# Holding VectorE and ScalarE to program order through the projections of a hybrid decoder step

## The chip, the cores and the metric

One core of one Trainium2 chip runs the whole program in one launch. The metric is the device time of one execution in microseconds. TensorE (PE in the profile; PEld is its weight load) multiplies, VectorE (DVE) and ScalarE (ACT) do element work, SyncE (SP) issues nearly all DMAs.

## The reference

One layer of a hybrid decoder on 288 tokens: 256 of a prompt and 32 of eight sample requests (four tokens each, with 2048 cached positions). Cut to what matters here:

```python
u = rmsnorm(h, g_mix)
z = u @ w_in                                   # 2048 x 2880
c_q, c_kv, k_r, x_br, y_br = split(z)          # 512, 256, 64, 1024, 1024
q = (rmsnorm(c_q, g_q) @ w_uq)                 # 8 heads of 128 + 64
o_lat = attend(q_lat, rope(q_r), rmsnorm(c_kv, g_kv), rope(k_r))   # prompt: causal; sample: paged cache
o_mla = o_lat @ w_uv
xc = causal_conv(x_br);  o_rec = rglru(xc);  o_lru = gelu(y_br) * o_rec
h = h + concat(rmsnorm(o_mla, g_out_mla), rmsnorm(o_lru, g_out_lru)) @ w_o
h = h + hier_moe(rmsnorm(h, g_ffn))            # 32 experts, 2 of them for each token
h = h + sigmoid(rmsnorm(h, g_ple) @ w_ple_gate) * (p @ w_ple_proj)
```

All in float32.

## The kernel before

Activations lie with the feature in the partitions and the 288 tokens along the free axis. A projection in `dense3` makes one block of 128 output columns. It goes through the 2048 (or 1024) rows in pieces of 8 x 128, called **steps** here. A step's weights, 128 x 1024 numbers, come by one DMA of 512 KB into `wraw` (4 buffers). To keep the product nearly exact, both sides are held in two parts. `load_split` makes the weights' parts:

```python
nc.scalar.copy(hi[:, x, :], r[:, x, :])                                   # L222: whi, 3 buffers
nc.vector.tensor_sub(lo[:, x, :], r[:, x, :], hi[:, x, :].bitcast(F32))   # L223: wlo, 2 buffers
```

`mm3` then issues three matmuls for each of the 8 row blocks: L232 (whi by the high part, h), L233 (whi by the low part, g), L234 (wlo by the high part, l). A step has 24 matmuls; it can begin with whi alone, and its first L234 needs wlo. After the last step of a block `evac` takes the sum out of PSUM, and after each step `hook()` runs.

The projections come in this order: `w_in` in 23 blocks of two steps (4 for `cq`, 3 for `lat` and `kr`, then for each of four LRU parts 2 for `xx` and 2 for `yb`), `w_uq` in 6 steps (each with two sums of 12 matmuls), `w_o[0]` (the recurrent half) in 16 steps and `w_o[1]` (the attention half) in 16 steps. That is 84 steps. Everything else of the layer is put between them by `hook()`: it pops one entry of the list `hooks` and then calls `tick()`, which moves each running **lane** on by one stage. Hooks hold the norms of the queries (`norm_q1`, `norm_q2`), the conv, gates, decay and scan of the LRU parts (`begin`, `conv`, `gates`, `decay`, `input`, `scan`, `out`), and in `w_o[1]` the routing's sums (`post`). Lanes are the 16 units of the sample attention (`sample`: scores, maximum, exp, transposes, output) beside the LRU blocks, and then `prompt_pool` and the 8 heads of the prompt attention (`prompt`) beside `w_o[0]`. `rsqrt_of` and `spread` make a per-token scale: `ssx`, `rsv`, `rss`, `rsr`, `diag`, `spread`, then `rx` (or `ry`, `ro`). `heads_out` splits the 8 heads' outputs (`om`) into parts before `w_o[1]`.

What decides the order: the program is traced, and a scheduler then lays each engine's instructions into one fixed row by its own estimates of time, subject to the dependencies. So the row of an engine needn't be the order in which the code was written: before, the casts of the weights (L222) and the subtractions (L223) stand among the hook's work wherever the scheduler put them. On the chip each engine goes through its row strictly in order, and an instruction that waits holds up all that stand behind it.

After the projections come the routing and the experts (MoE), from about 450 us on, whose weights stream through five and more slots of 2 MB each; SP issues the loads of weights in the order of its own row.

Of the kernel before, what the change touches and what calls it, by code (L numbers as in the profile page):

```python
# [117 lines left out]
def hymba_kernel(ctx, tc, a):  # L118
    nc = tc.nc
# [62 lines left out]
    def tick():  # L182

        for g in list(lane):
            if next(g, 1):
                lane.remove(g)
        for _ in range(min(PAGES // 4, len(loads))):
            loads.pop(0)()
        if queue:
            clock[0] += 1  # L190
            if clock[0] <= AHEAD or (clock[0] - AHEAD) % PACE == 0 or clock[0] >= DENSE:
                start()

    def start():
        if queue[0][0] and lane:
            return
        g = queue.pop(0)[1]()
        lane.append(g)
        if next(g, 1):
            lane.remove(g)  # L200

    def hook():
        if hooks:
            hooks.pop(0)()
        tick()

    def load(src, n=1):
        r = wps[0].tile([128, 8, 128], F32, name="wraw", bufs=wps[1])
        for i in range(n):
            dma(r[:, 8 * i // n:8 * (i + 1) // n, :],  # L210
                src[:, 1024 * i // n:1024 * (i + 1) // n].rearrange("p (k c) -> p k c", c=128))
        return r
# [23 lines left out]
    def dense3(srcs, xh, xl, evac, pre=(), ps_=None):  # L236

        acc = (ps_ or psA)([128, NTOK], "acc")
        nq = len(pre) if srcs is None else srcs.shape[0]
        last = 8 * nq - 1  # L240
        for q in range(nq):
            r = pre[q] if q < len(pre) else None
            hi, lo = r if isinstance(r, tuple) else load_split(None if r is not None else srcs[q], r)
            for k in range(8):
                kk = 8 * q + k
                mm3(acc, hi[:, k, :], lo[:, k, :], xh(kk), xl(kk), kk == 0, kk == last)
            if q == nq - 1:
                evac(acc)
            hook()
# [78 lines left out]
    for k in range(KD):  # L328
        if k in at:
            i, h = at[k]  # L330
# [5 lines left out]
    def squares(q):  # L336
        if q == 0:
            tc.keep_in_program_order(nc.scalar.activation(acc4, xT[:, :4, :], AF.Square))
        else:
            sq4 = xs.tile([128, 4, NTOK], F32, name="sq4")  # L340
            tc.keep_in_program_order(nc.scalar.activation(sq4, xT[:, 4 * q:4 * q + 4, :], AF.Square))
            nc.vector.tensor_add(acc4, acc4, sq4)
        if q == 3:
            nc.vector.tensor_add(acc4[:, 0:2, :], acc4[:, 0:2, :], acc4[:, 2:4, :])
            nc.vector.tensor_add(accs[0], acc4[:, 0, :], acc4[:, 1, :])
            st_x.close()
# [31 lines left out]
    def ev_q(i, p):  # L378
        nc.vector.tensor_mul(cq[:, i, :], p, rx_of())
        add_sq(accs[1], tmp, cq[:, i, :], i)  # L380

    pcq = []
    hooks += [lambda: None] * NSQ + [lambda q=q: squares(q) for q in range(4)]
    hooks += [lambda: [ev_q(i, pcq[i]) for i in range(2)], lambda: [ev_q(i, pcq[i]) for i in range(2, 4)]]
    for i in range(4):
# [472 lines left out]
    while hooks:  # L858
        hook()
# [20 lines left out]
    while lane or queue:  # L880
        hook()
# [828 lines left out]
```

## Time and profile before

| | |
|---|---|
| median of 3 runs | 1489.26 us (1486.46 to 1492.16) |
| the profiled execution | 1484.32 us, its span 1482.4 us |
| mean granted clock of TensorE | 0.957 |
| PE busy | 1302.5 us, 88% of the span |
| VectorE busy | 562.0 us, 38% |
| ScalarE busy | 397.7 us, 27% |
| mean DMA rate | 350 GB/s |

The span runs from the first to the last instruction. Busy shares are averages over stages: the projections take the first 449 us, and the MoE and the gated embedding the rest. Granted clock 1.00 is the full level, 2.4 GHz; a stretch below it was in part at the half level, 1.2 GHz.

### The profile page before, as it was taken

The page shows a single profiled execution, that of the slowest core. Times are in us where ns is not written, and L with a number is a line of the kernel's source. Part 1 is how long each engine was busy: PE and PEld are TensorE (multiplying, and loading weights), DVE is VectorE, ACT ScalarE, POOL GpSimd, SP SyncE. Part 2 cuts the span into 40 slices and gives each one's busy share as a digit, 9 for nine tenths or more (in the row PEclk, how much of TensorE's full clock was granted, in tenths as well). Part 3 has the DMA queues.
Part 4 walks back from the last instruction along what each step waited for, and adds up shares of the span by engine and source line. Part 5 has one row for each costly group of instructions (what it writes and reads, how often), then busy time and mean ns, then how long its engine had stood idle before and what let it go on. Part 6 is the DMA issues. An engine that isn't in the chain of part 4 may idle for free. (4 is left out here: it accounts for less than half of the span.)

```text
span 1482.4 us, 24470 instructions
## 1 busy us (share of the span) xinstructions
PE 1302.5 (88%) x9883; PEld 857.6 (58%) x9883; DVE 562.0 (38%) x1368; ACT 397.7 (27%) x762; POOL 3.0 (0%) x9
## 2 busy tenths in 40 slices
PE   8999888899999999679778777969788999999996
PEld 7997676788996445125224322516245666666786
DVE  6765644767653011000000010103024455555676
ACT  6545533655441101001000010102013322222236
POOL 0000000000000000000000000000000000000000
PEclk9999999999999999999989988989899999999997
DMA  7879776342768899999999999999999999999971
GB/s 273 286 241 363 259 268 215 118 165 86 263 257 334 347 414 427 428 426 430 427 428 427 428 427 426 418 423 428 416 420 419 420 418 419 418 419 418 412 310 65
DMA packets 81784, 518.34 MB, mean 350 GB/s; under 512 B 9473, under 2 KB 11714, under 8 KB 50818
## 3 DMA queue, kind: packets, MB, share of 16 engines
q1 hardware_dynamic: 81010, 514.33, 86.3%
q0 software_dynamic: 656, 2.39, 0.4%
q8 instruction: 80, 1.31, 0.4%
q14 instruction: 38, 0.31, 0.1%
HBM read 513.81 MB, written 2.88 MB: 349 GB/s over the span
## 5 line engine op out<-in xcount | busy, mean ns | idle before, releaser
L1119 PE MATMUL Gp<-w,Xq 128*32 128x512 f32 (+1 forms) x1888 | 339.4, 668 | 78.5 <-DMA w<-in_w_gate 40.0
L1119 PEld LDWEIGHTS Gp<-w,Xq 128*32 128x32 f32 (+1 forms) x1888 | 84.0, 126 | 280.1 <-issue 160.6
L232 PE MATMUL acc<-uh,whi 128*128 128x288 f32 x496 | 154.6, 312 | 10.6 <-ACT whi L228 5.7
L234 PE MATMUL acc<-uh,wlo 128*128 128x288 f32 x496 | 152.1, 307 | 8.2 <-DVE ms L541 5.2
L233 PE MATMUL acc<-ul,whi 128*128 128x288 f32 x496 | 150.6, 304 | 0.4 <-DVE ul L267 0.4
L1128 DVE SCALAR_TENSOR_TENSOR Yb<-Gp,rs,Yb 128x512 f32<-128x512 f32 x10 | 7.5, 751 | 329.6 <-PE Gp L1119 288.9
L1152 PE MATMUL Y<-w,w 128*32 128x256 f32 (+2 forms) x1440 | 112.4, 360 | 20.8 <-DMA w<-in_w_down 20.8
L1169 DVE TENSOR_TENSOR hT<-hT,yp 128x288 f32<-128x288 f32 x160 | 71.4, 450 | 155.3 <-PE yp L1167 155.1
L1092 PE MATMUL xp<-Pq,hn 96*128 96x256 f32 (+1 forms) x576 | 119.3, 359 | 8.4 <-DVE Pq L1076 8.4
L1092 PEld LDWEIGHTS xp<-Pq,hn 96*128 96x128 f32 x576 | 96.8, 196 | 49.6 <-issue 39.4
L232 PEld LDWEIGHTS acc<-uh,whi 128*128 128x128 f32 x496 | 95.6, 193 | 17.7 <-ACT whi L222 5.7
L223 DVE TENSOR_TENSOR wlo<-wraw,whi 128x1024 fp32r<-128x1024 f32 x82 | 99.9, 1218 | 12.3 <-PE acc L234 6.8
L234 PEld LDWEIGHTS acc<-uh,wlo 128*128 128x128 f32 x496 | 95.7, 193 | 14.8 <-DVE wlo L223 11.2
L222 ACT CAST whi<-wraw 128x1024 fp32r<-128x1024 f32 x82 | 85.1, 1045 | 68.1 <-PE acc L233 60.5
L233 PEld LDWEIGHTS acc<-ul,whi 128*128 128x128 f32 x496 | 96.0, 194 | 2.2 <-DVE ul L267 1.3
L1152 PEld LDWEIGHTS Y<-w,w 128*32 128x32 f32 (+1 forms) x1440 | 54.9, 115 | 64.4 <-DMA w<-in_w_down 34.3
L1156 ACT ACTIVATE Yh<-Y,wsl 128x256 fp32r<-128x256 f32 (+1 forms) x90 | 40.6, 451 | 182.9 <-PE Y L1152 182.2
L1096 DVE TENSOR_SCALAR Xq<-xp,P 128x256 f32<-128x256 f32 (+1 forms) x48 | 21.1, 439 | 161.5 <-PE xp L1092 161.5
L1152 PE MATMUL Y<-w,wl 128*32 128x256 f32 (+3 forms) x864 | 71.4, 360 | 6.2 <-DMA w<-in_w_down 6.2
L1127 ACT ACTIVATE Yb<-Gp,rs 128x512 f32<-128x512 f32 x10 | 6.9, 687 | 259.5 <-PE Gp L1119 259.4
L234 PE MATMUL acc<-gh,wlo 128*128 128x288 f32 x240 | 70.8, 295 | 1.4 <-DVE wlo L229 1.4
L233 PE MATMUL acc<-gl,whi 128*128 128x288 f32 x240 | 70.9, 295 | 0.0
(482 smaller groups left out, 1882.2 us busy)
## 6 DMA issues: line engine op xcount, KB each, us to landing
w<-in_w_gate SPq DMA_DIRECT2D x63, 2048.0 KB, 28.8
w<-in_w_down SPq DMA_DIRECT2D x112, 1024.0 KB, 17.4
w<-in_w_up SPq DMA_DIRECT2D x55, 2048.0 KB, 27.8
kv<-in_cache SPq DMA_DIRECT2D x128, 288.0 KB, 5.4
wraw<-in_w_in SPq DMA_DIRECT2D x44, 512.0 KB, 5.7
hT<-in_w_up SPq DMA_DIRECT2D x9, 2048.0 KB, 29.6
wraw<-in_w_o SPq DMA_DIRECT2D x32, 512.0 KB, 3.4
wraw<-in_w_pg SPq DMA_DIRECT2D x32, 512.0 KB, 17.4
```

The costliest lines, as they stand in the source:

```text
L222: nc.scalar.copy(hi[:, x, :], r[:, x, :])
L223: nc.vector.tensor_sub(lo[:, x, :], r[:, x, :], hi[:, x, :].bitcast(F32))
L232: nc.tensor.matmul(out, hi, xh, start=start, stop=False)
L233: nc.tensor.matmul(out, hi, xl, start=False, stop=False)
L234: nc.tensor.matmul(out, lo, xh, start=False, stop=stop)
L1092: nc.tensor.matmul(xp, hn[:, t, d * 128:(d + 1) * 128], Pq[:, t, :n], start=t == 0, stop=t == 2)
L1096: nc.vector.tensor_scalar(X[:, d, :n], xp, prm("g_ffn", d), None, op0=ALU.mult)
L1119: nc.tensor.matmul(acts[j][sl * e:sl * e + sl, :], X[:, kk, o:o + sl], wt[e](k), start=kk == 0, stop=kk == KD - 1)
L1128: nc.vector.scalar_tensor_tensor(sg, acts[1], rs, sg, op0=ALU.mult, op1=ALU.mult)
L1152: nc.tensor.matmul(Y[sl * e:sl * e + sl, :], at[:, f, sl * e:sl * e + sl], w(f), start=f == 0, stop=f == 3)
L1156: nc.scalar.activation(Yh, Y, AF.Copy, scale=ws)
L1169: nc.vector.tensor_add(h_, h_, yp)
```

## The change

A new function `in_order()` is called at the end of every `hook()`. It goes through the instructions that were traced since its last call, and gives each one on ScalarE or VectorE a dependency (without a semaphore) on the one traced before it on the same engine. A call with `first=True` before the first projection starts the chain. No instruction is added, removed or altered (762 on ScalarE, 1368 on VectorE, both before and after); the two engines' rows are held to the order of the code from the first step of `w_in` to the last hook of `w_o[1]`. TensorE's and SP's rows stay with the scheduler, which lays them by what it now finds. Lines of the changed kernel are numbered 15 or 16 higher (L222 is L237, L223 is L238, L874 is L890).

```diff
+    kept, traced = {}, [0]
+
+    def in_order(first=False):
+
+        ins = nc.cur_bb.bb.instructions
+        if not first:
+            for i in ins[traced[0]:]:
+                if i.engine in (mybir.EngineType.Activation, mybir.EngineType.DVE):
+                    if i.engine in kept:
+                        tc.add_manual_dep(i, kept[i.engine].name, mybir.DependencyInfo(
+                            mybir.DependencyClass.NoSync, mybir.DependencyReason.DATA), reason="in_order")
+                    kept[i.engine] = i
+        traced[0] = len(ins)
+
     def hook():
         if hooks:
             hooks.pop(0)()
         tick()
+        in_order()
...
     pcq = []
+    in_order(True)
     hooks += [lambda: None] * NSQ + [lambda q=q: squares(q) for q in range(4)]
```

Three places show what moves. The first is VectorE's row in the middle of `w_o[1]`, two steps long (`evt` and `hT` take a block's sum out, `acch` adds squares). Before:

```order
L874 TENSOR_TENSOR evt<-acc,ro 128x288
L223 TENSOR_TENSOR wlo<-wraw,whi 128x1024
L875 TENSOR_TENSOR hT<-hT,evt 128x288
L276 TENSOR_TENSOR acch<-acch,sqa 128x288
L874 TENSOR_TENSOR evt<-acc,ro 128x288
L223 TENSOR_TENSOR wlo<-wraw,whi 128x1024
```

And of the change:

```order
L890 TENSOR_TENSOR evt<-acc,ro 128x288
L891 TENSOR_TENSOR hT<-hT,evt 128x288
L291 TENSOR_TENSOR acch<-acch,sqa 128x288
L238 TENSOR_TENSOR wlo<-wraw,whi 128x1024
L890 TENSOR_TENSOR evt<-acc,ro 128x288
L891 TENSOR_TENSOR hT<-hT,evt 128x288
```

Before, `wlo` stood right behind `evt`; now `hT` and `acch` stand between them, and `wlo` is the last of its step.

The second is ScalarE's row at the seventh to eleventh step of `w_in`, where the token scale `rx` is made, the blocks of `cq` are taken out and normed (`sqa`, `qh`). Before:

```order
L222 CAST whi<-wraw 128x1024 x3
L257 ACTIVATE rss<-rsv 96x3
L297 COPY rx<-spread 128x288
L222 CAST whi<-wraw 128x1024
L272 ACTIVATE acc_103<-cq 128x288
L275 ACTIVATE sqa<-cq 128x288 x3
L222 CAST whi<-wraw 128x1024
```

And of the change:

```order
L237 CAST whi<-wraw 128x1024
L272 ACTIVATE rss<-rsv 96x3
L312 COPY rx<-spread 128x288
L287 ACTIVATE acc_103<-cq 128x288
L290 ACTIVATE sqa<-cq 128x288
L237 CAST whi<-wraw 128x1024
L290 ACTIVATE sqa<-cq 128x288 x2
L237 CAST whi<-wraw 128x1024
```

Before, two more casts stood ahead of `rss`; now the next step's cast stands behind `rss`, `rx` and the squares of `cq`.

The third is VectorE's row beside the LRU blocks, where a step's sum is taken out (`xx`), a sample unit goes on (`Obs`, `ms`) and the next part of the conv begins (`xc`, `cvs`, `cvp`). Before:

```order
L223 TENSOR_TENSOR wlo<-wraw,whi 128x1024
L741 TENSOR_TENSOR xx<-acc,rx 128x256
L742 TENSOR_TENSOR xx<-acc,rx 128x8x4
L570 SCALAR_TENSOR_TENSOR Obs<-Obs,ms,Os 128x256
L762 COPY cvs<-xx 128x48
L763 COPY cvp<-xx 128x6
L528 TENSOR_REDUCE ms<-Ss 128x1
L767 TENSOR_SCALAR xc<-xx,P 128x312
L530 TENSOR_TENSOR ms<-ms 128x1
L770 SCALAR_TENSOR_TENSOR xc<-xx,P,xc 128x312
L541 TENSOR_SCALAR ms<-ms 128x1
L223 TENSOR_TENSOR wlo<-wraw,whi 128x1024
```

And of the change:

```order
L238 TENSOR_TENSOR wlo<-wraw,whi 128x1024
L757 TENSOR_TENSOR xx<-acc,rx 128x256
L758 TENSOR_TENSOR xx<-acc,rx 128x8x4
L586 SCALAR_TENSOR_TENSOR Obs<-Obs,ms,Os 128x256
L544 TENSOR_REDUCE ms<-Ss 128x1
L546 TENSOR_TENSOR ms<-ms 128x1
L557 TENSOR_SCALAR ms<-ms 128x1
L564 SCALAR_TENSOR_TENSOR ms<-ms 128x1
L238 TENSOR_TENSOR wlo<-wraw,whi 128x1024
```

Before, the conv's first operations stood ahead of `wlo`, and the last `ms` of the unit (L548) behind it; now the sample unit's whole chain of `ms` stands ahead of `wlo` and the conv behind it, ahead of the next step's `wlo`.

## Rows read from the trace of the kernel before

**Rows 1.** Busy time, clock and DMA by stage; first a stretch and its length.

```profile
core 0: us, PE busy (x) PEld busy (x) DVE busy (x) ACT busy (x) POOL busy (x), PEclk, DMA share, GB/s
34.00:84.50 50.50, 50.09 (x365) 48.10 (x364) 34.48 (x69) 28.00 (x60) 0.00 (x0) 1.00 0.81 275
95.10:289.70 194.60, 174.69 (x1539) 136.52 (x1531) 111.02 (x280) 90.18 (x149) 0.00 (x0) 0.97 0.71 247
309.20:384.80 75.60, 75.60 (x513) 69.28 (x513) 49.28 (x110) 36.88 (x85) 0.00 (x0) 0.98 0.28 95
449.20:520.00 70.80, 66.63 (x408) 36.58 (x407) 14.99 (x73) 9.33 (x20) 0.00 (x0) 0.95 0.91 360
520.00:1482.40 962.40, 815.93 (x6171) 453.61 (x6167) 268.52 (x667) 164.29 (x342) 2.79 (x5) 0.94 0.97 405
```

**Rows 2.** The page's chain that ended last, and its two costliest weight-part groups.

```profile
DMA w<-in_w_down 22%; DMA w<-in_w_up 2%; PE Gp L1119 2%; PE xp L1092 2%; PE Y L1152 2%; DMA wpp<-in_w_pp 1%; PE s L1507 1%; PE acc L1516 0%; DVE hT L1613 0%; PE pp L1328 0%; PE yp L1167 0%; PE acc L234 0%; PE spread L293 0%; DVE z L1527 0%; PE acc L233 0%
...
L223 DVE TENSOR_TENSOR wlo<-wraw,whi 128x1024 fp32r<-128x1024 f32 x82 | 99.9, 1218 | 12.3 <-PE acc L234 6.8
...
L222 ACT CAST whi<-wraw 128x1024 fp32r<-128x1024 f32 x82 | 85.1, 1045 | 68.1 <-PE acc L233 60.5
```

**Rows 3.** Timeline of one step's end in `w_o[1]`: start, duration, instruction.

```profile
400.65 0.29 PE L234 MATMUL acc<-uh,wlo 128*128 128x288 f32 x1
...
400.98 0.46 DVE L874 TENSOR_TENSOR evt<-acc,ro 128x288 f32<-128x288 f32 x1 [1.06 <-PE acc L234]
401.36 1.22 DVE L223 TENSOR_TENSOR wlo<-wraw,whi 128x1024 fp32r<-128x1024 f32 x1
401.85 0.29 PE L234 MATMUL acc<-uh,wlo 128*128 128x288 f32 x1
402.25 0.29 PE L234 MATMUL acc<-uh,wlo 128*128 128x288 f32 x1
402.49 0.45 DVE L875 TENSOR_TENSOR hT<-hT,evt 128x288 f32<-128x288 f32 x1
```

**Rows 4.** The two evacuations of `w_o`: count, durations in ns, first and last start.

```profile
L874 DVE TENSOR_TENSOR evt<-acc,ry x16: 448/458/458, 309.0 to 384.4; 128x288 f32<-128x288 f32 x16
L874 DVE TENSOR_TENSOR evt<-acc,ro x16: 448/458/460, 392.4 to 448.9; 128x288 f32<-128x288 f32 x16
```

**Rows 5.** Timeline of a head's softmax beside `w_o[0]`, and its transposes one step apart.

```profile
319.75 0.49 PE L659 MATMUL pt<-C,Sb 128*128 128x128 f32 x3
326.72 0.49 PE L659 MATMUL pt<-C,Sb 128*128 128x128 f32 x3
...
322.18 0.56 DVE L645 TENSOR_TENSOR Sb<-S,C 128x384 f32<-128x384 f32 x1 [0.18 <-PE S L642]
324.84 0.55 DVE L655 TENSOR_SCALAR Sb<-Sb,m 128x128 f32<-128x128 f32 x2
```

**Rows 6.** Timeline of the token scale: its first and its last instruction.

```profile
35.55 0.15 DVE L256 TENSOR_SCALAR rsv<-ssx 96x3 f32<-96x3 f32 x1
38.16 0.40 ACT L297 COPY rx<-spread 128x288 f32<-128x288 f32 x1 [2.22 <-PE spread L293]
```

**Rows 7.** Groups by line and form, VectorE and ScalarE: count, busy us, mean ns.

```profile
L528 DVE TENSOR_REDUCE ms<-Ss 128x1 f32<-128x256 f32 x15 | 6.4, 423 | 8.8 <-PE Ss L523 8.8
L770 DVE SCALAR_TENSOR_TENSOR xc<-xx,P,xc 128x312 f32<-128x312 f32 x24 | 12.9, 539 | 0.1
L267 DVE SCALAR_TENSOR_TENSOR uh<-om,P,uh 128x256 fp32r<-128x256 f32 x8 | 3.9, 484 | 0.5 <-ACT uh L266 0.5
L542 ACT ACTIVATE Ssb<-Ss,ms 128x256 f32<-128x256 f32 x16 | 7.6, 475 | 38.8 <-DVE ms L541 34.3 <-DVE sp L723 4.4
L446 ACT COPY qrs<-qrT 64x32 f32<-64x32 f32 x16 | 3.5, 216 | 0.2
```

**Rows 8.** Two stretches of 10 us in which TensorE had gaps.

```profile
190.00:200.00 10.00, 8.23 (x66) 7.37 (x65) 4.24 (x11) 2.63 (x5) 0.00 (x0) 0.83 0.70 257
230.00:240.00 10.00, 6.66 (x63) 4.72 (x64) 3.28 (x10) 3.97 (x8) 0.00 (x0) 1.00 0.85 287
```

## The prediction

> **What bounds the kernel now.** I read the table by stage first, then the chain, then timelines inside the projections. The chain that ended last is made of the experts' weights (`w<-in_w_down` 22%) [rows 2]: behind the projections the span is set by a stream of weights, at 405 GB/s from 520 us on and 360 in the first 71 us [rows 1]. The projections are the other kind of stage. In their four large stretches TensorE is busy for 50.1 of 50.5, 174.7 of 194.6 and 75.6 of 75.6 us, while VectorE has 34.5, 111.0 and 49.3 and ScalarE less [rows 1]. So TensorE is the bound there, with some 20 us of idle time, nearly all of it beside the recurrent blocks. The work of the other engines is hidden, but only because it lies under matmuls: a step's 24 matmuls take 8 x 0.40 = 3.2 us (one L234 to the next is 402.25 - 401.85) [rows 3], and a step's own two weight operations take 1.05 + 1.22 us on two engines [rows 2].
>
> The timeline of a step's end [rows 3] shows how the cover is made. The last matmul is issued at 400.65, `evt` runs at 400.98, and `wlo` at 401.36 (two independent operations overlap by some 0.08 on VectorE). The next step's first L234 goes at 401.85, but this `wlo` ends at 402.58: the matmul reads a `wlo` that was made a step earlier, and the one at 401.36 is for the step after. So the weights' parts run a whole step ahead, in the second buffer, and `evt`, `hT` and `acch` hold up nothing.
>
> **What the change does to that.** Nothing is added. But in program order a step's weight parts stand behind all that the step before left: its evacuation, which waits for the last matmul, and its hook. The lead of a step is gone: `wlo` starts after the last matmul of the step before, however many buffers there are. TensorE can issue at most the next step's first pair (where `whi` isn't behind a wait itself) and then stands at the first L234 until `wlo` is done. The gap after a step is the time from its last matmul through that chain to `wlo`'s end; from the first L234 to the last there are then 7 x 0.40 = 2.8 us. What a gap costs is its length less what TensorE did in that place anyway.
>
> The terms, each against the same stretch of before:
>
> - **`w_o[1]`, 15 steps.** 0.33 to `evt` (400.98 - 400.65), then `evt` 0.46, `hT` 0.45, `acch` (the same size) 0.45, `wlo` 1.22 [rows 2, 3], less 0.05 of overlap: 2.86. With 2.8 a step takes 5.65. Before it took (448.9 - 392.4) / 15 = 3.77 [rows 4]. 15 x 1.88 = **+28**.
> - **Ahead of `w_o[1]`.** The 8 splits of `om` (0.48 each on VectorE [rows 7]) and the scale `ro` come in one lump after the last head; before, they lay under `w_o[0]`. 8 x 0.5 = 4, plus the scale's chain 38.16 - 35.55 = 2.6 [rows 6] of which a part was open before: **+5**.
> - **`w_o[0]`, 7 plain steps.** 0.33 + `evt` 0.46 + `hT` 0.45 + 1.22 = 2.4, and 2.8: 5.2 against 3.2: **+14**.
> - **`w_o[0]`, 8 steps with a head.** Before, one took 326.72 - 319.75 = 6.97 [rows 5], with TensorE always busy. After: 0.33, evacuation 0.9, then the head's softmax from `Sb` to its scaling, 322.18 to 325.39 = 3.2 [rows 5], then the casts that stand behind it on ScalarE (some 0.7 left over and `whi` 1.05) and `wlo` 1.22: 7.4, and 2.8 of matmuls: 10.2. The side matmuls lie in the gap. 8 x 3.2 = **+26**.
> - **Ahead of `w_o[0]`.** `prompt_pool`'s four weight splits stand in a lump ahead of the first step's: four times 1.05 + 1.22, partly overlapped and partly open before (from 289.7, the end of the blocks' stretch [rows 1], to the first `evt` at 309.0 [rows 4] it took 19.3 us). I take **+8**.
> - **LRU blocks, 16 blocks of two steps.** Before: 194.6 / 15 = 13.0 us a block, of which TensorE works 11.6 [rows 1]. In the step that ends a block the row holds: 0.33, the evacuation 0.6, `Obs` 0.5, the maximum 0.42, three small `ms` 0.5, exp 0.48 with its sum 0.2, `ms` on both engines 0.5 (the larger ones in [rows 7]), then `whi` 1.05 and `wlo` 1.22: 5.5. In half the blocks a conv of 4 x 0.54 [rows 7] with its gates, or the decay's input and scans, adds 2.6: 6.85 on average. The other step of a block costs 1.65. 2 x 2.8 + 6.85 + 1.65 = 14.1, 1.1 more than before; 15 times is 17, and `lru_const` (some twenty dependent small operations) 3: **+20**. The term is a small difference of large numbers, so 0 to 40.
> - **Start of that stage.** The chain `qls`, first scores, maximum, exp, `whi`, `wlo` stands serially before the first block, and the cached pages are loaded later, since the clamp of the table now waits behind the last `wlo` of `w_uq`: **+7.5** (3 to 15).
> - **`w_in` from the seventh step and `w_uq`.** After the seventh step: sum, scale 2.6 and its copy 0.4 [rows 6], two `cq`, two squares, `whi`, `wlo`: 7.2; after the tenth the norm of `cq` (four multiplications and splits): 10; after the fourteenth the scale of the latents, rope and transposes: 7.8; two lighter ones of 3.5. In `w_uq` two steps hold two ropes each (copy, matmul, three operations of 0.45, four small copies of 0.22 [rows 7], twice, before the next `whi`): 10.6 a step against about 4; four steps with `qn` take 5.8. From 34 us to the end of `w_uq` that makes 94.5 where before it took 50.5: **+44**. Before, no gap is there to fill (50.1 of 50.5 busy [rows 1]).
>
> Sum: 28 + 5 + 14 + 26 + 8 + 20 + 7.5 + 44 = **+153**. Lower ends, where each chain's independent operations overlap and the side matmuls fill what they can: `w_o[1]` with its head 27, `w_o[0]` with its head 40, the blocks 0, their start 3, the stretch to the last `qn` 36: **+106**. Upper ends: 36, 56, 40, 15 and 50: **+197**.
>
> **The clock.** The stretch of 190 to 200 us, where TensorE was busy for 8.2 of 10, shows 0.83, but 230 to 240, with 6.7 of 10, shows 1.00 [rows 8]: idle time of 2 to 3 us in 10 doesn't bring the clock down each time. No stretch of before shows a gap of 5 to 10 us, and the change will have some, with about 30 of over 3 us. A stretch of 10 us at 0.83 lacks 1.7 us of full clock. If none of the 30 leads to such a stretch the cost is 0, if all do it is 50; I take +15, nearer the low end, by the row of 230 to 240. The Trainium skill, "TensorE: Matmul & The Clock Gate", section "What's actually happening", says that throttled is the default state and that activity releases the throttle. By that rule the change's long gaps would each bring the low level back, which is the second rival below; the row of 230 to 240 bears it out only in part.
>
> **What lies behind.** The experts' first weights fill their slots before the projections end in either kernel, and then wait for slots. A later end of the projections moves the rest one to one. At most the 71 us at 360 GB/s against 405 (8 us) could come back [rows 1]; I take nothing.
>
> **Sum for the execution.** 1484 (the profiled one) + 153 + 15 = 1652; the median of before is 5 above its profiled execution, so 1657, and I forecast **1660 us**.
>
> **Rivals.**
>
> 1. **The gaps are partly hidden** (17 in 100). If the lower ends hold, above all in the blocks, where TensorE's 11.6 us a block leave 1.4 free already and much of its work is a sample unit's, which can fill the gap, the sum is +106 with no clock's cost: 1489 + 106 = 1595, give or take 20. For it: the 1.4 us a block. Against it: a unit's matmuls wait for the same chain of `ms` and exp that `wlo` waits for.
> 2. **The clock falls after most long gaps** (18 in 100). Then 30 stretches lose 1.7 each and the steps of `w_o`, each with its own gap, lose as much again at most: +50 to +100 in place of 15, 1695 to 1745. For it: 0.83 where TensorE was idle for less than 2 of 10 us [rows 8]. Against it: the second stretch there.
> 3. **Faster** (2 in 100). The waits that TensorE has beside the recurrent blocks go away since `wlo` no longer stands behind an unfinished softmax chain, and the other steps keep their cover, because the evacuation could wait on a sum finished early (three PSUM buffers). This would give back at most the 20 us: 1468. It decides if `wlo` of a step can start before the last matmul of the step before. In the change's row it stands behind that step's `evt`, so it can only in the half of the steps that end no block; the chance is small.
> 4. **No change that can be measured** (3 in 100): the gaps appear but the weight stream behind absorbs them. It would need the slots to be empty at the MoE's start and 150 us of catching up; 8 are there.
>
> The central case has 60 in 100, with 1630 to 1695. The range that leaves out no more than 2 in 10 takes in two thirds of either neighbour: **1585 to 1725**. A difference of under 0.5%, some 7 us, is about what can't be told from no change here: faster 0.02, same 0.03, slower 0.95.
>
> **What would show it.** In the profile after, the step of `w_o[1]` from `evt` to `evt` should be 5.4 to 5.9 us, with `wlo` starting 1.6 us after the last matmul; TensorE idle by some 150 us more before the MoE, most of it put down to `wlo` or `whi`; the last `qn` near 128 us, the last `yb` near 361, the last `evt<-acc,ry` near 504, and the last `evt<-acc,ro` near 602, each later by what the clock costs; from there to the end the same 1033 us as before. I'm wrong if a step of `w_o[1]` stays near 4 us (then `wlo` is not bound to the evacuation), if the granted clock in `w_o` falls to 0.8 or less, or if the MoE gets shorter by more than 10 us.

## The result and the profile after

The changed kernel takes 1733.81 us (median of 4 runs, 1731.97 to 1740.39) where the kernel before takes 1488.57: 1.166 times as long, interval 1.164 to 1.168. The forecast was 1660, its range ended at 1725. The sign was right, and so was the mechanism of the gaps; the cost of the clock was not. The change costs 245 us where 171 was forecast.

The profiled execution has a span of 1730.2 us and a granted clock of 0.903 (before 0.957). Here is its table by stage, cut at the same events of the program: the first `xx`, the last `yb`, the first and last `evt<-acc,ry`, the last `evt<-acc,ro`.

```profile
core 0: us, PE busy (x) PEld busy (x) DVE busy (x) ACT busy (x) POOL busy (x), PEclk, DMA share, GB/s
34.00:167.60 133.60, 90.08 (x476) 78.47 (x478) 39.43 (x77) 31.61 (x65) 0.00 (x0) 0.77 0.35 118
167.60:411.90 244.30, 197.53 (x1529) 150.45 (x1527) 113.69 (x290) 82.23 (x137) 0.00 (x0) 0.88 0.58 197
411.90:454.30 42.40, 24.77 (x116) 18.58 (x116) 17.74 (x40) 15.84 (x26) 0.00 (x0) 0.76 0.33 119
454.30:594.10 139.80, 104.01 (x515) 90.07 (x514) 50.50 (x110) 38.41 (x89) 0.00 (x0) 0.79 0.17 57
594.10:693.90 99.80, 73.91 (x521) 65.25 (x521) 43.42 (x80) 29.54 (x48) 0.00 (x0) 0.95 0.48 181
693.90:1730.20 1036.30, 886.36 (x6571) 491.59 (x6570) 284.25 (x741) 173.22 (x361) 2.78 (x5) 0.94 0.96 399
```

The same cut through the trace of before gives 60.8, 194.6, 19.6, 75.4, 64.5 and 1033.5 us, with TensorE busy for 60.4, 174.7, 18.6, 75.4, 63.7 and 882.9. By how much each stage is longer, and how much of that is idle time of TensorE (length less busy time) and how much is busy time for the same matmuls:

| stage | longer by | idle more | busy more | forecast, gaps |
|---|---|---|---|---|
| `w_in` from the seventh step, `w_uq`, start of the LRU blocks | 72.8 | 43.1 | 29.7 | 51.5 |
| LRU blocks | 49.7 | 26.9 | 22.8 | 20 |
| ahead of `w_o[0]` | 22.8 | 16.6 | 6.2 | 8 |
| `w_o[0]` | 64.4 | 35.8 | 28.6 | 40 |
| ahead of `w_o[1]`, and `w_o[1]` | 35.3 | 25.1 | 10.2 | 33 |
| sum | 245.0 | 147.5 | 97.5 | 152.5 |
| all behind | 2.8 | -0.7 | 3.5 | 0 |

The idle column answers to the forecast of the gaps, 148 against 153. The busy column answers to what the forecast had as "the clock", at 15. Nothing comes back behind the projections.

The granted clock of the table says how much of the busy column is the clock's. Each stage's length times what its clock lacks of 1.00 adds up to 105 us over the five stages of the projections, where before it was 7. So TensorE was at the half level for some 210 us there; laid over the trace's records of the clock, it was busy for 170 of these (before 14). At the half level work takes at most twice as long (the pitches below are 0.24 and 0.13 us), so up to 85 us were lost, before 7: up to 78 of the 97 (an estimate).

The signs that the prediction named came in part. A step of `w_o[1]` takes 5.74 us, `wlo` starts 1.6 us after the last matmul, and what lies behind is unchanged. But the granted clock of `w_o[0]` is 0.79, which had been named as a sign of being wrong. And most of the idle time was to end with `wlo` or `whi`; of 169 us of TensorE's waits from 34 to 694 us these two end 53:

```profile
PE acc L247 <- ACT whi L237: 32.0, 18, 7.0
PE tp L570 <- ACT Ssb L558: 29.9, 13, 5.0
PE acc L249 <- DVE wlo L238: 21.1, 35, 2.2
PE S L657 <- ACT kn L653: 19.4, 7, 3.6
```

Each line has the us in total, the count and the longest. `Ssb` is the exp of the sample attention and `kn` the keys of a head, both made on ScalarE. 18 waits are for `whi`: where a cast on ScalarE stands behind a norm, a rope or the splits of `yb`, it is `whi` and not `wlo` that is late. The longest, 7.0 us, stands behind the norm of the queries.

The mechanism is seen best in `w_o[1]`, where [rows 3] showed the step before. VectorE's timeline over one step of the changed kernel:

```profile
642.28 0.46 DVE L890 TENSOR_TENSOR evt<-acc,ro 128x288 f32<-128x288 f32 x1 [3.29 <-PE acc L249]
642.78 0.46 DVE L891 TENSOR_TENSOR hT<-hT,evt 128x288 f32<-128x288 f32 x1
643.15 0.45 DVE L291 TENSOR_TENSOR acch<-acch,sqa 128x288 f32<-128x288 f32 x1
643.52 1.22 DVE L238 TENSOR_TENSOR wlo<-wraw,whi 128x1024 fp32r<-128x1024 f32 x1
648.02 0.46 DVE L890 TENSOR_TENSOR evt<-acc,ro 128x288 f32<-128x288 f32 x1 [3.28 <-PE acc L249]
```

The step is 648.02 - 642.28 = 5.74 us, forecast 5.65. TensorE in the same step, the side matmuls and the first and last of the step's L249, the matmuls that read `wlo` (L234 before):

```profile
643.29 0.70 PE L940 MATMUL lg<-wr,hT 128*96 128x36 f32 x6 [0.78 <-DVE hT L891]
643.82 0.51 PE L946 MATMUL tph<-C,hT 128*96 128x128 f32 x3
644.79 0.40 PE L249 MATMUL acc<-uh,wlo 128*128 128x288 f32 x1 [0.46 <-DVE wlo L238]
...
647.69 0.29 PE L249 MATMUL acc<-uh,wlo 128*128 128x288 f32 x1
```

VectorE now stands idle for 3.3 us until the last matmul. TensorE then has the next step's first pair and the side matmuls to do, and otherwise stands idle until VectorE has been through `evt`, `hT`, `acch` and `wlo`. The two engines take turns.

And the clock, at one step of the second half of `w_o[0]`. TensorE's timeline around one gap:

```profile
586.67 0.29 PE L247 MATMUL acc<-ul,whi 128*128 128x288 f32 x1
586.80 0.29 PE L248 MATMUL acc<-ul,whi 128*128 128x288 f32 x1
586.94 0.29 PE L249 MATMUL acc<-ul,wlo 128*128 128x288 f32 x1
589.40 0.61 PE L249 MATMUL acc<-ul,wlo 128*128 128x288 f32 x1 [2.18 <-DVE wlo L238]
589.81 0.44 PE L247 MATMUL acc<-ul,whi 128*128 128x288 f32 x1
590.05 0.44 PE L248 MATMUL acc<-ul,whi 128*128 128x288 f32 x1
```

Ahead of the gap the matmuls go at 0.13 us each, behind it at 0.24, and one lasts 0.44 in place of 0.29. Of the recorded matmuls of the projections 483 of 1850 have the next one behind them at 0.2 to 0.32 us, where before it was 144 of 1849. What this adds to the pitch of 0.132 is 51 us against 14: 37 us of the 97 are slow projection matmuls by this count alone, without the side matmuls.

What the level costs shows in two neighbouring steps of `w_o[0]` with the same work, a head each. The first was at the half level for a good part, the second at the full level:

```profile
490.30:504.70 14.40, 11.55 (x47) 9.64 (x46) 4.42 (x12) 3.35 (x9) 0.00 (x0) 0.64 0.10 36
504.70:514.70 10.00, 7.17 (x47) 6.14 (x46) 4.43 (x11) 3.24 (x9) 0.00 (x0) 1.00 0.17 55
```

TensorE is idle for 2.8 us in both. It is busy for 4.4 us more in the first, and the step is 4.4 us longer.

### The profile page after: what moved, and what is told of

Same layout as the page of the kernel before. It is cut to its first block, busy times and chain, and to the rows that moved or that the text cites. A ratio compares the mean times of both kernels' runs of the same rounds, so it can differ in the third digit from the quotient of the medians.

```text
span 1730.2 us, 24474 instructions
## 1 busy us (share of the span) xinstructions
PE 1402.2 (81%) x9883; PEld 918.6 (53%) x9883; DVE 570.0 (33%) x1368; ACT 390.9 (23%) x757; POOL 3.0 (0%) x9
## 5 line engine op out<-in xcount | busy, mean ns | idle before, releaser
L247 PE MATMUL acc<-uh,whi 128*128 128x288 f32 x496 | 161.6, 326 | 25.0 <-ACT whi L237 17.0
L249 PE MATMUL acc<-uh,wlo 128*128 128x288 f32 x496 | 163.7, 330 | 11.7 <-DVE wlo L238 11.5
L248 PE MATMUL acc<-ul,whi 128*128 128x288 f32 x496 | 165.1, 333 | 0.1
L247 PEld LDWEIGHTS acc<-uh,whi 128*128 128x128 f32 x496 | 104.9, 212 | 36.2 <-ACT whi L237 26.1
L249 PEld LDWEIGHTS acc<-uh,wlo 128*128 128x128 f32 x496 | 104.3, 210 | 28.0 <-DVE wlo L238 19.5
L238 DVE TENSOR_TENSOR wlo<-wraw,whi 128x1024 fp32r<-128x1024 f32 x82 | 100.1, 1223 | 50.6 <-ACT whi L237 48.7
L248 PEld LDWEIGHTS acc<-ul,whi 128*128 128x128 f32 x496 | 111.5, 225 | 1.0 <-DVE ul L282 0.6
L237 ACT CAST whi<-wraw 128x1024 fp32r<-128x1024 f32 x82 | 84.3, 1038 | 16.8 <-PE acc L248 16.8
L249 PE MATMUL acc<-gh,wlo 128*128 128x288 f32 x240 | 70.8, 295 | 1.4 <-DVE wlo L244 1.4
L247 PE MATMUL acc<-gh,whi 128*128 128x288 f32 x240 | 70.3, 293 | 0.0
```

The source lines that it names most:

```text
L247: nc.tensor.matmul(out, hi, xh, start=start, stop=False)
L248: nc.tensor.matmul(out, hi, xl, start=False, stop=False)
L249: nc.tensor.matmul(out, lo, xh, start=False, stop=stop)
```

## The experiments

**The order held in one stage alone.** `in_order()` chains only while a flag is set, and the flag is set from one place in the program to the next:

```diff
-        if not first:
+        if not first and keep[0]:
...
+    in_order(not keep[0])
+    keep[0] = True            # or False, ahead of the LRU, w_o[0] and w_o[1]
```

> The order is held only from the first step of w_in to the end of w_uq; the rest is left to the scheduler. In the changed kernel the first xx came 73 us later than before. Theory 1 (each stage loses its own lead of a step, and the clock falls where its own gaps are long): the cost is local, the first xx comes 60 to 75 us later than before, the stages behind take what they took before, time near 1555 (1545 to 1565). Rival (a late start lets loads run ahead and gives back time in the stages behind, or it disturbs them): the stages behind differ by over 10 us, time under 1535 or over 1575.

> The order is held only from the LRU constants to the first step of w_o[0] (this takes in the sample lanes and what the hooks left over ahead of w_o[0]). Changed kernel: 50 us more from the first xx to the last yb, and 22 more to the first evt of w_o[0]. Theory 1: both come back here, +55 to +75, time 1540 to 1565. Rival (these stages were long only because pages and weights came late after the first stage): +25 or less, under 1515.

> The order is held only from the first step of w_o[0] to the splits of the heads' outputs, ahead of w_o[1]. Changed kernel: 65 us more between the first and last evt of w_o[0], 7 more to the first evt of w_o[1]. Theory 1: head steps of 10 us at full clock and longer ones at the low level, +55 to +75, time 1540 to 1565. Rival (the clock falls here only because the stage before left TensorE idle for long): head steps of 10 us throughout, +40 to +48, near 1530.

> The order is held only in w_o[1]; the splits of the heads' outputs stay under w_o[0]. Theory 1: a step goes from 3.8 to 5.7 us at a clock of 1.00, 15 x 1.9 = +28, time 1512 to 1520. Rival (the scheduler's row of TensorE or the loads matter more than the two held rows): a step stays under 4.5 us, +10 or less.

Measured, one run each beside 1489.79 us of the kernel before: 1566.71, 1572.35, 1546.14 and 1523.75. The excesses are 76.9, 82.6, 56.4 and 34.0, together 250, against 245 for the whole change. So the losses add up. The places inside were not all as expected, and single runs leave some us open. In the first run the first `xx` comes at 149.9, 55 us later than before and not 73, and the LRU blocks behind it, whose order is free, take 221 us in place of 194.6. A stage behind that differs by over 10 us was its rival's condition, though the time is not the rival's, and so the sum of 250 is partly luck. For the first 50 of these the DMA rate is 383 GB/s, where before the stage's mean was 247 [rows 1]: loads that a late head left over. That these loads make the 26 us was not tried. The time is 2 us above its range. The second run is 7 us above its range: the lump ahead of `w_o[0]` takes 50.7 us there (yb at 349.4, first evt at 400.1). The third shows head steps of 10.0 to 15.3 us though TensorE had no long idle time in the stage ahead, which speaks against its rival. In the fourth 13 of 15 steps take 5.4 to 5.7 us, and the other two more than 7; it is 4 us above its range.

**One engine alone.**

```diff
-                if i.engine in (mybir.EngineType.Activation, mybir.EngineType.DVE):
+                if i.engine in (mybir.EngineType.DVE,):      # or Activation
```

> Only VectorE is held to program order; ScalarE stays with the scheduler. Theory 1 (what costs is that wlo stands behind the evacuation and the hook on VectorE): most of the loss stays, less one cast of 1.05 us where whi stood behind a hook on ScalarE (some 40 places); 1650 to 1710. Rival (the chains through both engines' rows cost, and one free row breaks them): under 1600.

> Only ScalarE is held to program order; VectorE stays with the scheduler. Theory 1: no loss in w_o[1], where no cast stands behind a wait for the last matmul, and losses where a cast stands behind the exps, the rsqrt chain or the ropes: 1520 to 1580. Rival (either row alone loses the lead, since wlo needs whi): over 1620.

1697.38 and 1573.67 beside 1490.59 (one run each), as expected: VectorE's row alone makes 207 of the 245 us, ScalarE's alone 83. That the sum is more than 245 would follow if in many places the two stand behind the same wait; this was not tried. Two things were not as expected with ScalarE held and VectorE free. The blocks beside the LRU take 174 us, 21 less than before, while the stage to the first `xx` takes 61 more; why was not looked into. And `w_o[1]` loses too, its steps going by turns at 3.2 and 6.8 us. The scheduler made VectorE's row anew, and in the part that I looked at two evacuations stand there ahead of one `wlo`.

**The parts a step ahead in program order.** Both rows are held as in the change, but the code makes the parts of the next step before the matmuls of this one:

```diff
+    def ahead():
+        if todo:
+            ready.append(load_split(todo.pop(0)))
...
-            hi, lo = r if isinstance(r, tuple) else load_split(None if r is not None else srcs[q], r)
+            hi, lo = pre[q] if q < len(pre) else ready.pop(0)
+            if q or not pre:
+                ahead()
```

> The order is held on both engines as in the change, but the code makes the parts of the next step before the matmuls of this one, so that wlo stands a step ahead in program order too (same buffers). Theory 1 (the lost lead is the cause, not the fixed order): w_o[1] back to 3.8 to 4.0 us a step, clock back, gaps only where a hook lasts longer than a step; 1495 to 1550. Rival (the fixed order of the hooks' chains is the cause): over 1600.

That run took the columns of `w_in` in another order than the blocks need. Its 20101.83 us are of a layer that computes something else and say nothing; only its projections can be read, and they ended 96 us later than before, so the expected 1495 to 1550 was missed already there. It was made again with the right order:

> As in the run before under the name ahead, with the sources of the weights in the order of use (that run took the columns of w_in in another order, so what it computed and its time behind the projections mean nothing; its projections ended 96 us later than before). Theory 1 in its first form (the lost lead of one step is the whole cause): under 1550. In a second form (a lead of one step covers an evacuation, but not the hooks whose chains last longer than a step; there the parts of the step after next still stand behind the whole chain): w_o[1] and the plain steps of w_o[0] as before, and 80 to 100 us lost in the head, the LRU blocks and the lumps: 1570 to 1590. Rival (the fixed order of the hooks alone): over 1620.

1578.56 us (2 runs), 1.061 times before, interval 1.055 to 1.066, some 8 us either way: the second form. VectorE's timeline in `w_o[1]`:

```profile
505.06 0.46 DVE L901 TENSOR_TENSOR evt<-acc,ro 128x288 f32<-128x288 f32 x1 [0.51 <-PE acc L249]
505.55 0.46 DVE L902 TENSOR_TENSOR hT<-hT,evt 128x288 f32<-128x288 f32 x1
505.93 0.46 DVE L301 TENSOR_TENSOR acch<-acch,sqa 128x288 f32<-128x288 f32 x1
507.31 1.23 DVE L238 TENSOR_TENSOR wlo<-wraw,whi 128x1024 fp32r<-128x1024 f32 x1 [0.93 <-ACT whi L237]
509.05 0.46 DVE L901 TENSOR_TENSOR evt<-acc,ro 128x288 f32<-128x288 f32 x1 [0.51 <-PE acc L249]
```

The row reads exactly as that of the changed kernel, `evt`, `hT`, `acch`, `wlo`, and the step is back at 3.99 us: this `wlo` is for the step after next. That `wlo` stands last costs nothing; that it is for the very next step costs 1.75 us a step (5.74 less 3.99). `w_o[0]` is back at 75.7 us too. Most of what is left lies in the stage to the first `xx` (98.8 in place of 60.8), beside the LRU (219.6 in place of 194.6) and in the lump ahead of `w_o[0]` (38.9 in place of 19.6).

**All held but the weights' parts, and nothing held but the parts ahead.** In the first of these `load_split` notes its instructions, and `in_order()` passes them over; the second is the kernel before with the edit above.

```diff
-                if i.engine in (mybir.EngineType.Activation, mybir.EngineType.DVE):
+                if i.engine in (mybir.EngineType.Activation, mybir.EngineType.DVE) and i.name not in wparts:
```

> All instructions of both engines are held to program order but the weights' parts, which the scheduler may put anywhere among them. Theory 1 (the place of the parts is what costs): 1485 to 1510. Rival (the serial order of the hooks' chains costs by itself, about the 80 to 96 us that a lead of one step leaves): 1560 to 1590.

> No order is held; the code makes the parts of the next step before the matmuls of this one, and the scheduler lays all rows. Theory 1: the scheduler gives the parts a lead already, so there is little to win, 1480 to 1495. If the code's order still weighs in its choice, some of the 20 us of waits beside the LRU blocks go: 1470 to 1482.

With the parts free 1532.12 us, 1.029 times before (1.026 to 1.032): between the two expectations, and neither theory's. The steps of `w_o[0]` and `w_o[1]` are as before. 25 of the 51 us by which the profiled execution is longer lie in the lump ahead of `w_o[0]`: it still takes 45 us, at a low clock:

```profile
309.30:354.30 45.00, 33.79 (x134) 25.08 (x135) 16.64 (x41) 16.54 (x29) 0.00 (x0) 0.58 0.31 111
```

With nothing held and the parts ahead in the code, 1489.01 us, 1.000 times before (0.999 to 1.001). The scheduler gave the parts their lead already, and there is nothing to win.

**The clock.** The changed kernel with matmuls that nothing reads, for TensorE to do in the gaps:

```diff
-        acc = (ps_ or psA)([128, NTOK], "acc")
+        bank = (ps_ or psA)([128, 512], "acc")
+        acc = bank[:, :NTOK]
...
+            for _ in range(wn):
+                nc.tensor.matmul(bank[:, NTOK:], onr[:, :128], onr[:, :512 - NTOK], start=False, stop=False,
+                                 skip_group_check=True)
```

> The changed kernel with matmuls added that nothing reads (128 x 224, 10 at the head of a step of w_in from the fourth block on, 20 in a step of w_uq, 16 in one of w_o[0], none in w_o[1]); they write to columns of the sum's bank that aren't used, so that TensorE has something to do in the gaps. Theory 1 (gaps plus a clock that falls in them): clock near 1.00 in w_o[0] where it was 0.79, its head steps all near 10 us, time 1670 to 1700. Rival (the low level costs next to nothing because slow matmuls only fill gaps): the clock rises but the time stays at 1725 or above; or the added work makes it longer.

In this first run the added matmuls carried the start and stop flags, and the sums beside them were spoilt, so only its stages are read. 1740.24 us: the rival's time. The clock rose (0.95 in `w_o[0]`, where it was 0.79), the last steps of `w_o[0]` went from 6.9 to 5.4 us, and the LRU blocks took 13 us more. That many of the added matmuls stood there where there was no gap is a likely reason, not a shown one. The next had the flag off and kept to `w_o[0]`:

> The changed kernel with 16 matmuls that nothing reads (128 x 224, into columns of the sum's bank that aren't used) at the head of each step of w_o[0], and nowhere else. In the first run of this kind the last steps of w_o[0] took 5.4 us with such matmuls in their gap, where the changed kernel took 6.9 at a clock of 0.7 to 0.8. Theory 1 (the gap costs twice: its own length and a lower clock behind it): the stage from first to last evt goes from 140 to 125 to 131 us, time 1718 to 1726. Rival (the clock costs nothing there): 1733 or more.

1734.87 us (2 runs, 1729.92 to 1739.82), ratio 1.166 (1.161 to 1.171): the rival's time, and no gain that can be measured. The stage took 136 us in place of 140, not the 125 to 131 expected. The last five steps took 5.4 us each and gained 6 us together; the two ahead of them took 7.3 and 7.0 in place of 5.7 and lost 3; the steps with a head took the same in sum (94.8 against 95.4). Then only places where nothing but projection matmuls stands on either side of the gap:

> The changed kernel with matmuls that nothing reads in the undivided gaps of two places: 16 at the head of each of the last seven steps of w_o[0], 10 in the first half of each step of w_uq. Theory 1 (the clock falls behind an undivided gap and costs time): the last steps of w_o[0] go from 6.9 to 5.4 us, the last four of w_uq from 7 to about 5.8, some 10 us in all, ratio to before 1.155 to 1.160. Rival (slow matmuls only fill gaps, the work added is only added): 1.166 or more.

1725.11 us (4 runs), ratio 1.158 (1.156 to 1.161), against 1.166 (1.164 to 1.168) without: the added work makes the kernel 11 us faster, as expected, 4 us either way by the two intervals. The profiled executions differ by 5.0 us: the two edited stages are 3.1 and 4.8 us shorter, and others move by up to 4 us either way. The table for two of these steps, the changed kernel first (13.7 us from 580.4) and then this one (10.8 us from 572.2):

```profile
580.40:594.10 13.70, 9.40 (x44) 8.94 (x44) 4.08 (x6) 0.00 (x0) 0.00 (x0) 0.75 0.23 77
```

```profile
572.20:583.00 10.80, 10.54 (x84) 10.07 (x83) 4.11 (x6) 0.43 (x1) 0.00 (x0) 1.00 0.30 97
```

The clock is 1.00 in place of 0.75, the step 5.4 us in place of 6.9. So the gap costs twice there, by its own length and by the level at which the matmuls behind it run. The expectation had called these gaps undivided; that is so for the last two steps of `w_o[0]`, while the first two slow ones have a gap of 1.00 and one of 0.65 us, with a pair of matmuls between.

> The same, and 8 such matmuls at the head of the first step of each block beside the LRU. Theory 1: the clock of that stage rises from 0.88 towards 0.95 and it loses 5 to 15 us of its 244; ratio to before 1.145 to 1.157. Rival (in that stage the added matmuls stand ahead of the sample unit's scores and delay its chain by as much as the clock gives back): the stage keeps its 244 us or gets longer while its clock rises; ratio as in the other run or above.

1725.52 us (1718.41 to 1737.46), ratio 1.162 (1.156 to 1.168): it doesn't tell the theories apart. The blocks beside the LRU took 241 us in its profile, 3 less than the changed kernel, but so they did in the run before it, which adds nothing there; the clock of the stage was 0.89 in both.

## Why the prediction was right and wrong, step by step

- **The lead of a step is lost, and TensorE waits for a chain on VectorE in its place**: shown, by the timelines of `w_o[1]` and by the run with the parts a step ahead, which undoes 155 of the 245 us with both rows still held. Which wait ends a gap was foreseen less well: `whi` and `wlo` end 53 of 169 us, and TensorE's own side matmuls, which wait for the hooks' chains, most of the rest.
- **Each stage's gaps**: their sum was right, 148 us of idle time against 153, but partly by luck: the stages miss by 4 to 9 us each, three below the forecast and two above it. `w_o[1]` (a step of 5.74 against 5.65) and the steps of `w_o[0]` at full clock (10.0 against 10.2 with a head, 5.4 against 5.2 without) were worked out from rows of a few operations, and hold. The lump ahead of `w_o[0]` was mis-sized by half (+8 forecast, 16.6 of idle time and 22.8 in all). It had been taken for four weight splits of `prompt_pool`. The run with the parts free still holds these (they are not made by `load_split`), with the scale `ry` and the splits of `yb`, and there the serial order of them makes it 45 us by itself, TensorE busy for 34 of these at 0.58 in place of 19. The LRU term (+20) was 27 of idle time; the rows listed for its block's last step add up to 5.8 us and not to the 5.5 written, which would have made the term 4 us larger. In the stage to the first `xx` idle time was 43 in place of 51.5: 36 up to the last `qn`, at 142.3 us, against 44, and 7 behind it against 7.5.
- **The clock, +15, 0 to 50**: this is the step that failed. The busy time of TensorE in the projections rose by 97 us with the same matmuls, up to 78 of it work at the half level. Where steps with the same work can be set side by side, the whole rise lengthens the step: 4.4 us in a head step of `w_o[0]` (a clock of 0.64 against 1.00) and 1.5 us in a plain one (6.89 against 5.36). 37 us are slow projection matmuls by their pitch, and 11 us were got back by filling gaps in two places. The rest of the 97, some 19 us, was not settled; the modelled end of a burst's last matmul, shown with 0.29 us where the pitch is 0.13, will have a part in it. The step leaned on the row of 230 to 240 us in [rows 8], a stretch that kept 1.00 with 3.3 us idle, and priced a low stretch at 1.7 us, behind fewer than one in three of some 30 long gaps. Of gaps of 3 us and more there are 14 in the changed kernel's projections, not 30, and at the end of 13 of them TensorE was at the half level; of gaps of 1 to 3 us there are 37, and it was so at the end of 10. Before, there were 9 gaps of 1 us and more, none of 3. The second rival had this mechanism at 1695 to 1745, with 18 in 100; the measured time lies in it, though its count of long gaps was twice too high. By the Trainium skill, "TensorE: Matmul & The Clock Gate", section "What's actually happening", the throttled state is the default that activity has to release, and the rows around the gap of 2.18 us agree with that: 0.13 us a matmul ahead of it, 0.24 behind. The steps of `w_o[1]`, at 1.00 behind a gap of 0.78 and one of 0.46, show that not every gap brings it.
- **What lies behind moves one to one**: right, 1036.3 us against 1033.5, nothing came back.
- **My first account of the cause was too simple.** A lead of one step gives back 155 us, making the parts' place wholly free gives back another 46 (1578.56 to 1532.12), and 43 us stay with the hooks' order alone (1532.12 against 1488.79). That the serial chains cost by themselves, the rival in the runs with the parts ahead and free, is so far true, for less than a fifth of the loss.

## What to carry to other kernels

When a row is put into program order, look for what was prepared a step early in it, and ask which step's operand an instruction makes: a row that reads the same can be for the next step or the one after, and in `w_o[1]` that was 1.75 us for every step. When a change opens gaps on TensorE, price each gap twice, once for its length and once for slower matmuls behind it, from rows that show a matmul's pitch on either side of a gap, and count gaps of 1 us too.

## What was not expected of the hardware

The same gaps went with either clock. In `w_o[1]` TensorE is idle for 0.78 and 0.46 us a step, with side matmuls between, and the granted clock stays at 1.00:

```profile
642.00:654.00 12.00, 9.51 (x70) 8.30 (x69) 5.08 (x9) 3.73 (x6) 0.00 (x0) 1.00 0.28 89
```

In the run with `w_o[1]` alone held the same steps, with the same gaps, take 5.4 to 5.7 us each but for two, and one of these two, from 418.1, has the same gaps too and takes 7.3 us, at 0.78 from 419.4 to 427.0. In the second half of `w_o[0]` of the changed kernel a step with a gap of 1.00 and one of 0.64 us takes 5.4 us, and the next two, with the same gaps, 6.9; in the last two the gap is 2.18 in one piece, at 0.75. What decides between the levels was not tried. And work that nothing reads, put into gaps, made the kernel faster by 11 us.
